# A decoder layer on one core: w_out staged four blocks at a time, gates in 32 rows, and loads read in the source's order

## The chip, the cores and the metric

The kernel runs on one core of a Trainium2 chip. It is one launch that computes one decoder layer for a prompt of 1024 tokens and for 8 single new tokens. The metric is the device time of one execution in microseconds, the median of the runs that were made. The core has a matmul engine (TensorE, PE in the profile, with its weight loads as PEld), three other compute engines (VectorE or DVE, ScalarE or ACT, GpSimd or POOL), and a queue of transfers that SyncE issues (SP). GpSimd issues transfers as well.

## The reference

The layer is `x = x + W_out(concat[RG-LRU branch, mLSTM branch])`, then a final norm. Both branches read the same normalised input through one projection `w_in` of 1024 to 7176 columns.

```
hn = rmsnorm(x, g_norm);  u = hn @ w_in
xa, za, uq, uk, uv, uo, zb, ui, uf = split(u)
yA, hA, bufA = rglru_branch(xa, ...)                  # conv of 4 taps, two gates, a scan over time
hB, C, n, m  = mlstm_seq(q, k, v, ig, lf, C0, n0, m0) # 4 heads, chunks of 128 tokens
yB = headnorm(sigmoid(uo) * hB) * g_mhead
merged = concat([yA * silu(za), yB * silu(zb)])
x = x + merged @ w_out;   y = rmsnorm(x, g_final)

# inside one chunk of the mLSTM, per head
b = cumsum(lf);  D = b_t - b_s + ig_s (causal);  g = b + m
m_t = max(g, max_s D);  w = exp(D - m_t);  P = w * (q k^T)
num = P v + exp(g - m_t) * (q C)
C_new = exp(b_L + m - m_L) * C + sum_s exp(b_L - b_s + ig_s - m_L) k_s v_s^T
```

The gate values `ig` and `lf` are one number for each token and head. From them come, for each token, the running maximum m and the factors that the chunks use. All in float32; the decode tokens do the same with one step from a given state of 8 x 4 matrices of 256 x 256.

## The kernel before

A float32 value is split into a high and a low part (`split`, lines 68 to 71: ScalarE copies the high part, VectorE subtracts it), and a product of two such values is three matmuls (`mm3`, lines 62 to 66). The order of the work in the source is written out by hand; a planner then places the instructions of each engine by the readiness it reckons for them, so an instruction can stand earlier in its engine's queue than in the source. A tile is released when its last reader is done, and a load into a reused tile waits for that.

**Projection.** `w_in` is worked through in 14 units (`UNITS`) of two 256-column blocks. Each unit is seven products (a Strassen-like scheme, `Q_P1` to `Q_P4`) of combinations of the input, kept in 14 slots of 128 x 2 x 1024 floats (`big(0)` to `big(13)`, two for each product), with combinations of the weights that `prep` makes in a ring of six tiles (`ws`). A product has two parts (`product` yields after each); after each part `pop_bg` runs a step of background work: the gates, the RG-LRU branch (`rgq`), the decode state updates (`dcq`). In the last unit the slots of a product come free as the product ends.

**Gates.** `gates` (lines 524 to 627) loads the parameters, takes log-sigmoids, and transposes the gate values of all tokens into 4 rows (heads) of 1024. Two scans along the row give the running maximum and, with a mask that restarts every 128 columns, the sums within a chunk. Four more row sets are stacked in a 128 x 1024 tile `stk` at rows 0, 32, 64 and 96 and transposed back eight times (L617). The factor between chunks goes to DRAM (`d_cs`) and is read back to all partitions. `d_alpha` holds a row for each head; each chunk and head later loads its piece to all partitions as W.

**Decode states.** `decode_steps` loads a state matrix C and a row v for each token and head, scales C on ScalarE (L881), adds the new outer product on VectorE (L883), and stores it.

**w_out and the output stage.** w_out is 16 blocks of 128 rows by 1024 columns, 0.5 MB each. `wo_load(n)` loads blocks n and n+1 into the `ws` ring. `wo_prep(n)` multiplies them with the decode rows (L1204, into `dec_o`) and splits them into the slot with the block's number (blocks 14 and 15 into the two raw tiles of the projection). Blocks 8 to 15 are scaled by `gm4` on the way (L1213, L1214). `wo_due` asks for blocks 0 to 7 after products 0 to 3 of the last unit; the rest is asked for in the code after the units and in the first steps of the output stage. There, 28 steps n (chunk and head) each run `m_k` (mask and exponent of W, splits), `m_a`, `m_b`; `fill` puts pieces of the output product (`out_part`, six or twelve matmuls a piece) between them. `o_load` loads the transposed RG-LRU rows rh and rl of a chunk.

Of the kernel before, what the change touches and what calls it, by code (L numbers as in the profile page):

```python
# [17 lines left out]
P = 128  # L18
# [31 lines left out]
def hymba_kernel(  # L50
# [17 lines left out]
    def split(hi, lo, src):  # L68

        A.copy(hi, src)  # L70
        V.tensor_tensor(lo, src, hi.bitcast(F32), op=ALU.subtract)  # L71

# [77 lines left out]
    d_alpha = dram.tile([NH, T], F32, name="d_alpha")  # L150
    d_cs = dram.tile([NH, NCH], F32, name="d_cs")
# [372 lines left out]
    def gates():  # L524
# [9 lines left out]
        stk = fp.tile([P, T], F32, tag="stk", name="stk")  # L534
        msk = fp.tile([NH, T], F32, tag="msk", name="msk")
        G.memset(msk, 1.0)
        G.memset(msk.rearrange("p (c l) -> p c l", l=L)[:, :, 0:1], 0.0)
        G.memset(stk, 0.0)
        dgb = fp.tile([P, NB, 8], F32, tag="dgb", name="dgb")
        ld(dgb, d_gd.partition_broadcast(P))  # L540
        yield
# [13 lines left out]
        V.scalar_tensor_tensor(lg, fx, 0.0, lg, op0=ALU.min, op1=ALU.subtract)  # L555
        lf = lg[:, 0:32].rearrange("p (c h) -> p c h", h=NH)
# [6 lines left out]
        V.tensor_scalar(gm4, PT[:, :, R_GM], 0.25, None, op0=ALU.mult)  # L563

        dgm = fp.tile([P, 2, NB, NH], F32, tag="dgm", name="dgm")
# [11 lines left out]
        rows = fp.tile([NH, 2, T], F32, tag="rows0", name="rows0")  # L577
        lfr, igr = rows[:, 0, :], rows[:, 1, :]
        for half in range(2):
            for src, dst in ((lf, lfr), (gs, igr)):  # L580
                pr = ps("s" if dst is lfr else "qp", [NH, 512])
                for q in range(4):
                    TE.transpose(pr[:, q * P:(q + 1) * P], src[:, half * 4 + q, 0:NH], idF)
                V.tensor_copy(dst[:, half * 512:(half + 1) * 512], pr)
            yield
        rows1 = fp.tile([NH, 2, T], F32, tag="rows1", name="rows1")
        mr, br = rows1[:, 0, :], rows1[:, 1, :]
        V.tensor_tensor_scan(mr, lfr, igr, 0.0, op0=ALU.add, op1=ALU.max)
        V.tensor_tensor_scan(br, msk, lfr, 0.0, op0=ALU.mult, op1=ALU.add)
        yield  # L590
        al = lfr
        V.tensor_tensor(al, br, mr, op=ALU.subtract)
        ld(d_alpha, al)
        stq(p_m[0, 0].rearrange("(h o) -> h o", o=1), mr[:, T - 1:T])
        V.tensor_tensor(br, igr, br, op=ALU.subtract)
        c3 = lambda t: t.rearrange("p (c l) -> p c l", l=L)
        sm = fp.tile([NH, 3, NCH], F32, tag="gsm", name="gsm")
        mpv, aL, csr = sm[:, 0], sm[:, 1], sm[:, 2]
        G.memset(mpv, 0.0)
        V.tensor_copy(mpv[:, 1:NCH], c3(mr)[:, 0:NCH - 1, L - 1])  # L600
        V.tensor_copy(aL, c3(al)[:, :, L - 1])
        V.tensor_tensor(csr, aL, mpv, op=ALU.add)
        A.activation(csr, csr, AF.Exp)
        ld(d_cs, csr)
        ld(cs_b, d_cs.partition_broadcast(P))
        yield
        V.tensor_tensor(c3(stk[0:4]), c3(al), mpv.unsqueeze(2).to_broadcast([NH, NCH, L]), op=ALU.add)
        V.tensor_copy(stk[32:36], br)
        V.tensor_tensor(c3(stk[64:68]), c3(br), aL.unsqueeze(2).to_broadcast([NH, NCH, L]), op=ALU.add)
        V.tensor_scalar(stk[96:100], mr, -1.0, None, op0=ALU.mult)  # L610
        for _ in range(14):
            yield
        for half in range(2):
            pk = ps(("s", "qp")[half], [P, 4, P])
            for q in range(4):
                c = half * 4 + q
                TE.transpose(pk[:, q, :], stk[:, c * P:(c + 1) * P], idF)  # L617
            s = slice(half * 4, half * 4 + 4)
            V.tensor_copy(be_t[:, s, :], pk[:, :, 32:36])
            A.activation(gi_t[:, s, :], pk[:, :, 0:4], AF.Exp)  # L620
            A.activation(de_t[:, s, :], pk[:, :, 64:68], AF.Exp)
            A.activation(em_t[:, s, :], pk[:, :, 96:100], AF.Exp)
            yield
# [51 lines left out]
    def rg_unit(jj):  # L675
# [10 lines left out]
        if jj == 3:  # L686
            rgq.extend([rg_final, lambda: None, rg_rows])
# [175 lines left out]
    def decode_steps(h):  # L863
# [12 lines left out]
        def token(b):  # L876
            i = h * NB + b

            def f():
                vb_, C = ds_.pop(("v", i)), ds_["C", i]  # L880
                A.mul(C, C, dGI[:, b, h:h + 1])  # L881
                for kb in range(2):
                    V.scalar_tensor_tensor(C[:, kb, :], vb_, st["kw"][:, kb, b:b + 1], C[:, kb, :],  # L883
                                           op0=ALU.mult, op1=ALU.add)
# [130 lines left out]
    def m_load(n):  # L1015
# [5 lines left out]
        ld(W, d_alpha[h:h + 1, ts_].rearrange("o t -> (o t)").partition_broadcast(P))  # L1021
# [20 lines left out]
    def m_k(n):  # L1042
# [5 lines left out]
        V.scalar_tensor_tensor(W, W, be_t[:, c, h:h + 1], maskT, op0=ALU.add, op1=ALU.min)  # L1048
# [132 lines left out]
    wo = []  # L1181
    dec_o = []

    oraw = {}

    def wo_load(n):

        for m in (n, n + 1):
            oraw[m] = ws([P, T], f"oraw{m}", F32)
            ld(oraw[m], w_out[0, m * P:(m + 1) * P, :])  # L1190

    def wo_prep(n):


        if n == 0:
            dec_o.append(ps("tr", [P, 512]))
        if n not in oraw:
            wo_load(n)
# [146 lines left out]
    def wo_due(q):  # L1345

        if q < 4:
            bg.append(lambda: wo_prep(2 * q))
# [26 lines left out]
    for n, (u, q) in enumerate(seq):  # L1375
# [4 lines left out]
        if u == last_u:  # L1380
            wo_due(q)
# [136 lines left out]
```

## Time and profile before

| | |
|---|---|
| median of the runs | 960.22 us (960.17 to 962.28) |
| the profiled execution | 960.01 us, of which the span of its instructions 958.2 us |
| granted TensorE clock, mean | 0.999 |
| TensorE busy | 930.4 us (97% of the span) |
| VectorE, ScalarE, GpSimd busy | 714.4, 583.9, 146.3 us |
| moved by DMA | 153.71 MB, mean 160 GB/s |

Rows of a timeline give start, duration, engine, line, operation, tiles written and read, and in brackets the idle time of the engine before it with what ended it. A count such as x4 means that as many records stand in the row. A float32 matmul leaves two records. Matmuls overlap, so their pace is read from the distance of their starts. Rows of waits give the waiting instruction, what it waited for, the time in total, how often, and the longest. TensorE's busy time is modelled, so small losses between matmuls don't appear as idle.

### The profile page before, as it was taken

To read this page: it belongs to the slowest core of one execution; us is meant where nothing else is said; L and a number is where in the kernel's file an instruction comes from. 1 tells how busy PE (TensorE), PEld (TensorE's weight loads), DVE (VectorE), ACT (ScalarE), POOL (GpSimd) and SP (SyncE) were. 2 spreads that over 40 slices of the span, in tenths; PEclk is the share of its full clock that TensorE was granted. 3 is DMA by queue.
4 is the path that set the end of the run, shared out by engine and by line. 5 is a ranking of instruction groups with operands and counts; after the bars stand their busy time and mean duration, and the time that the engine had idled before them with its cause. 6 is when DMAs were issued, how large, how long until landed. Compare 5 with 4: busy or idle time off the path is not lost.

```text
span 958.2 us, 15403 instructions
## 1 busy us (share of the span) xinstructions
PE 930.4 (97%) x5370; PEld 760.4 (79%) x5370; DVE 714.4 (75%) x1482; ACT 583.9 (61%) x1044; POOL 146.3 (15%) x258
## 2 busy tenths in 40 slices
PE   7999989999999999999999999999989999999997
PEld 7897767777787988787789998866557888888886
DVE  6876898879787878989787757686556676676664
ACT  6553446768676857677678664465546466455633
POOL 1111112112212122112212221010200100000020
PEclk9999999999999999999999999999999999999999
DMA  6431347345745465466636362434873654564361
GB/s 193 143 122 43 132 140 253 115 171 195 250 145 198 159 204 173 163 200 210 206 115 225 116 206 85 157 110 148 288 222 93 200 165 121 158 183 135 113 114 47
DMA packets 131363, 153.71 MB, mean 160 GB/s; under 512 B 15798, under 2 KB 110038, under 8 KB 131278
## 3 DMA queue, kind: packets, MB, share of 16 engines
q1 hardware_dynamic: 113558, 96.86, 33.8%
q0 software_dynamic: 17728, 55.87, 16.5%
q8 instruction: 42, 0.69, 0.3%
q14 instruction: 35, 0.29, 0.1%
HBM read 101.11 MB, written 51.65 MB: 159 GB/s over the span
## 4 chain that ended last, share of the span: by engine, by line
PE 70%; DVE 11%; DMA 10%; ACT 4%; issue 4%; SPq 1%; POOL 0%; ACTq 0%; DVEq 0%; POOLq 0%
PE ps_o L66 12%; PE ps_o L64 12%; PE ps_o L65 12%; PE ps_kv L64 7%; PE ps_kv L66 7%; PE ps_kv L65 7%; DMA Cb<-in_state_mlstm_C_dram 2%; PE ps_tr L227 2%; DMA W<-d_alpha 2%; PE ps_s L738 1%; PE ps_s L1068 1%; DVE wl L71 1%; DMA raw<-in_w_in_dram 1%; PE ps_tr L1204 1%; DMA oraw<-in_w_out_dram 1%
## 5 line engine op out<-in xcount | busy, mean ns | idle before, releaser
L71 DVE TENSOR_TENSOR wl<-raw,wh 128x1024 fp32r<-128x1024 f32 x91 | 111.0, 1220 | 28.4 <-ACT wh L70 18.6
L70 ACT CAST wh<-raw 128x1024 fp32r<-128x1024 f32 x91 | 95.2, 1047 | 60.0 <-PE ps_o L65 16.6
L64 PE MATMUL ps_kv<-cb_hi,wh 128*128 128x512 f32 x320 | 128.3, 401 | 0.5 <-ACT s L308 0.3
L66 PE MATMUL ps_kv<-cb_hi,wl 128*128 128x512 f32 x320 | 125.7, 393 | 0.0
L65 PE MATMUL ps_kv<-cb_lo,wh 128*128 128x512 f32 x320 | 125.1, 391 | 0.0
L64 PE MATMUL ps_o<-cb_hi,wh 128*128 128x512 f32 x240 | 95.0, 396 | 0.0
L66 PE MATMUL ps_o<-cb_hi,wl 128*128 128x512 f32 x240 | 94.0, 392 | 0.0
L65 PE MATMUL ps_o<-cb_lo,wh 128*128 128x512 f32 x240 | 93.6, 390 | 0.0
L64 PEld LDWEIGHTS ps_kv<-cb_hi,wh 128*128 128x128 f32 x320 | 60.1, 188 | 24.5 <-issue 5.5
L66 PEld LDWEIGHTS ps_kv<-cb_hi,wl 128*128 128x128 f32 x320 | 60.1, 188 | 15.6 <-issue 2.5
L65 PEld LDWEIGHTS ps_kv<-cb_lo,wh 128*128 128x128 f32 x320 | 60.2, 188 | 11.7
L64 PE MATMUL ps_kv<-wh,cb_hi 128*128 128x256 f32 x192 | 55.3, 288 | 0.0
L64 PE MATMUL ps_o<-wo,rh 128*128 128x512 f32 (+1 forms) x136 | 53.5, 394 | 1.7 <-DMA rh<-d_rm 1.7
L65 PE MATMUL ps_kv<-wl,cb_hi 128*128 128x256 f32 x192 | 54.3, 283 | 0.0
L66 PE MATMUL ps_kv<-wh,cb_lo 128*128 128x256 f32 x192 | 54.3, 283 | 0.0
L64 PEld LDWEIGHTS ps_o<-cb_hi,wh 128*128 128x128 f32 x240 | 45.1, 188 | 10.9 <-issue 1.7
L66 PEld LDWEIGHTS ps_o<-cb_hi,wl 128*128 128x128 f32 x240 | 45.0, 188 | 10.6 <-issue 0.8
L64 PE MATMUL ps_o<-wo,mh 128*128 128x512 f32 (+1 forms) x136 | 52.8, 388 | 0.0
L66 PE MATMUL ps_o<-wo,ml 128*128 128x512 f32 (+1 forms) x136 | 52.0, 382 | 0.8 <-DVE ml L71 0.8
L65 PEld LDWEIGHTS ps_o<-cb_lo,wh 128*128 128x128 f32 x240 | 45.1, 188 | 9.2
L66 PE MATMUL ps_o<-wo,rl 128*128 128x512 f32 (+1 forms) x136 | 52.0, 382 | 0.1
L65 PE MATMUL ps_o<-wo,rh 128*128 128x512 f32 (+1 forms) x136 | 51.8, 381 | 0.0
(469 smaller groups left out, 2534.2 us busy)
## 6 DMA issues: line engine op xcount, KB each, us to landing
raw<-in_w_in_dram SPq DMA_DIRECT2D x56, 512.0 KB
Cb<-in_state_mlstm_C_dram SPq DMA_DIRECT2D x32, 256.0 KB
out_dram<-Cb POOLq DMA_DIRECT2D x32, 256.0 KB, 4.3
qk<-d_qk SPq DMA_DIRECT2D x32, 256.0 KB
oraw<-in_w_out_dram SPq DMA_DIRECT2D x16, 512.0 KB
d_qk<-s POOLq DMA_DIRECT2D x24, 256.0 KB, 3.7
x<-in_x_prompt_dram SPq DMA_DIRECT2D x8, 512.0 KB
d_x<-s POOLq DMA_DIRECT2D x16, 256.0 KB, 2.7
```

Of the source, the lines that this page charges most:

```text
L64: TE.matmul(out, ah, bh, start=first, stop=False, skip_group_check=True)
L65: TE.matmul(out, ah, bl, start=False, stop=False, skip_group_check=True)
L66: TE.matmul(out, al, bh, start=False, stop=last, skip_group_check=True)
L70: A.copy(hi, src)
L71: V.tensor_tensor(lo, src, hi.bitcast(F32), op=ALU.subtract)
L227: TE.matmul(pz[32 * g:32 * g + 32, :], hnd[:, k, :], raws[u, k // 4][:, k % 4, :], start=k < 4, stop=k >= 4, skip_group_check=True)
L738: TE.matmul(pg, w[:, n, :], st["xx"][n], start=k == 0, stop=k == 1)
L1068: TE.matmul(S, qk[:, 2 + kb, :], qk[:, kb, :], start=kb == 0, stop=kb == 1)
L1204: TE.matmul(dec_o[0][32 * g:32 * g + 32, :], md, oraw[m][:, half * 512:(half + 1) * 512], start=n == 0, stop=n == 14, skip_group_check=True)
```

## The change

Gates: the 8 chunks and 4 heads become 32 rows of 128 columns. Scans run within a row; the maximum is carried between chunks by four scans over 8 values on one row; two small matmuls with ones bring the carried maximum to the rows and the factor between chunks to all partitions, instead of the trip through `d_cs`. The stack is one 128 x 128 tile and one transpose. The steps are spread over 13 background steps, one after each part, where there were 26, two after each part.

w_out: blocks 0 to 11 are loaded four at a time into slots 0 and 1 (free after the first product of the last unit), blocks 12 to 15 into the `ws` ring. `wo_dec` multiplies several pairs with the decode rows in one go, `wo_split` splits a pair into the slots two above its number (12 and 13 into the raw tiles, 14 and 15 into slots 0 and 1). `wo_due` is called after every part of the last unit; the first `o_load` stands in it. Ahead of the output stage stand five `fill` pieces in place of four.

Order: `pin` ties an instruction to the one before it in the source on the same engine, so it can't be placed ahead of that one; no wait is added. It is put on the two decode state operations, on the mask of W, and on ScalarE's part of the w_out split. The final rows of the RG-LRU branch come two empty steps later.

```diff
+    pin = tc.keep_in_program_order
-    d_alpha = dram.tile([NH, T], F32, name="d_alpha")
-    d_cs = dram.tile([NH, NCH], F32, name="d_cs")
+    d_alpha = dram.tile([NCH * NH, L], F32, name="d_alpha")
...
+        lgi = fp.tile([P, 2, 32], F32, tag="lgi", name="lgi")
+        V.scalar_tensor_tensor(lgi[:, 0], fx[:, 0:32], 0.0, lg[:, 0:32], op0=ALU.min, op1=ALU.subtract)
+        V.tensor_copy(lgi[:, 1].rearrange("p (c h) -> p c h", h=NH), gs[:, :, 0:4])
...
+        R = NCH * NH
+        pr = ps("qp", [R, 2, P])
+        for n in range(2):
+            TE.transpose(pr[:, n, :], lgi[:, n, :], idF)
...
+        V.tensor_tensor_scan(ml, lfr, igr, NEG, op0=ALU.add, op1=ALU.max)
+        V.tensor_tensor_scan(br, ones[0:R, :], lfr, 0.0, op0=ALU.mult, op1=ALU.add)
...
-                for q in range(4):
-                    TE.transpose(pr[:, q * P:(q + 1) * P], src[:, half * 4 + q, 0:NH], idF)
-        V.tensor_tensor_scan(mr, lfr, igr, 0.0, op0=ALU.add, op1=ALU.max)
-        V.tensor_tensor_scan(br, msk, lfr, 0.0, op0=ALU.mult, op1=ALU.add)
+        for n, t in enumerate((ml, br)):
+            TE.transpose(pe[:, n, :], t[:, L - 1:L], idF[:R, :R])
...
+        for h in range(NH):
+            V.tensor_tensor_scan(mrow[:, 1:, h], ch_(er[:, 1])[:, :, h], ch_(er[:, 0])[:, :, h], 0.0, op0=ALU.add, op1=ALU.max)
...
+        TE.matmul(pc[0:R, 0:1], mrow[:, 0:NCH, :].rearrange("p c h -> p (c h)"), ones[0:1, 0:1], start=True, stop=True)
+        TE.matmul(pc[:, 32:64], ones[0:1, :], er[:, 2], start=True, stop=True)
+        V.tensor_copy(cs_b.rearrange("p h c -> p c h"), ch_(pc[:, 32:64]))
...
-                TE.transpose(pk[:, q, :], stk[:, c * P:(c + 1) * P], idF)
+        TE.transpose(pk.rearrange("p g c h -> p (g c h)"), stk, idF)
...
-            rgq.extend([rg_final, lambda: None, rg_rows])
+            rgq.extend([rg_final, lambda: None, lambda: None, lambda: None, rg_rows])
...
-                A.mul(C, C, dGI[:, b, h:h + 1])
+                pin(A.mul(C, C, dGI[:, b, h:h + 1]))
...
+                    pin(V.scalar_tensor_tensor(C[:, kb, :], vb_, st["kw"][:, kb, b:b + 1], C[:, kb, :],
+                                               op0=ALU.mult, op1=ALU.add))
...
-        V.scalar_tensor_tensor(W, W, be_t[:, c, h:h + 1], maskT, op0=ALU.add, op1=ALU.min)
+        pin(V.scalar_tensor_tensor(W, W, be_t[:, c, h:h + 1], maskT, op0=ALU.add, op1=ALU.min))
...
+    def wo_load(n, slot=None):
+        for i, m in enumerate((n, n + 1)):
+            if slot is None:
+                oraw[m] = ws([P, T], f"oraw{m}", F32)
+            else:
+                if i == 0:
+                    pair = big(slot, [P, 2, T], f"oraw{m}", F32)
+                oraw[m] = pair[:, i]
             ld(oraw[m], w_out[0, m * P:(m + 1) * P, :])
+    def wo_dec(ns, first=False, last=False):
+        ms = [n + i for n in ns for i in range(2)]
+        for m in ms:
             md = mAd[:, m, :] if m < 8 else mB[0][:, m - 8, :]
             for half in range(2):
+                g = 2 * (m % 2) + half
                 TE.matmul(dec_o[0][32 * g:32 * g + 32, :], md, oraw[m][:, half * 512:(half + 1) * 512], ...)
+    def wo_split(n):
...
+                t = big(m + 2 if m < 12 else m - 14, [P, 2, T], f"wo{m}")
...
+                pin(A.mul(t[:, 0], raw, gm))
...
+    def wo_due(i):
+        if i in (1, 6, 11):
+            for slot in range(2):
+                wo_load({1: 0, 6: 4, 11: 8}[i] + 2 * slot, slot)
+        if i == 4:
+            wo_dec((0, 2), True)
+            wo_split(0)
+        if i == 5:
+            wo_split(2)
+        if i == 9:
+            wo_dec((4, 6))
+            wo_split(4)
+        if i == 10:
+            o_load(0)
+            wo_split(6)
+        if i == 12:
+            wo_load(12)
...
-    o_load(0)
     m_k(4)
-    wo_load(10)
-    wo_prep(8)
+    wo_load(14)
     fill(2)
-    wo_load(12)
-    wo_prep(10)
-    fill(2)
+    wo_dec((8, 10, 12))
+    for n in (8, 12, 10):
+        wo_split(n)
+    o_load(1)
+    fill(3)
+    wo_dec((14,), last=True)
+    wo_split(14)
```

More of the change, by code (lines that the diff above doesn't have):

```diff
@@ L533, in gates @@
         ld(m0b, st_m[0].partition_broadcast(P))
[L534 to L538, printed above, removed]
         dgb = fp.tile([P, NB, 8], F32, tag="dgb", name="dgb")
         ld(dgb, d_gd.partition_broadcast(P))
+        yield
         yield
@@ L609, in gates @@
[L609 to L623, printed above, removed]
+        V.tensor_scalar(stk[0:R], al, mp[:, 0:1], None, op0=ALU.add)
@@ new lines, in gates @@
+        V.tensor_copy(stk[R:2 * R], br)
+        V.tensor_scalar(stk[2 * R:3 * R], br, al[:, L - 1:L], None, op0=ALU.add)
+        V.tensor_scalar(stk[3 * R:4 * R], ml, -1.0, None, op0=ALU.mult)
+        yield
+        yield
+        pk = ps("s", [P, 4, NCH, NH])
+        TE.transpose(pk.rearrange("p g c h -> p (g c h)"), stk, idF)
+        V.tensor_copy(be_t, pk[:, 1])
+        A.activation(gi_t, pk[:, 0], AF.Exp)
+        A.activation(de_t, pk[:, 2], AF.Exp)
+        A.activation(em_t, pk[:, 3], AF.Exp)
@@ L1206, in wo_prep @@
+    def wo_split(n):
         for m in (n, n + 1):
             raw = oraw.pop(m)
[L1208 removed]
+            if m in (12, 13):
+                t = rawp.tile([P, 2, T], F32R, tag=f"raw{m - 12}", name=f"wo{m}")
+            else:
+                t = big(m + 2 if m < 12 else m - 14, [P, 2, T], f"wo{m}")
+            wo[m] = t
             if m < 8:
[L1210 removed]
+                pin(A.copy(t[:, 0], raw))
+                V.tensor_tensor(t[:, 1], raw, t[:, 0].bitcast(F32), op=ALU.subtract)
```

96 lines of the change are left out of this document (36 added, 60 removed).

## The prediction

> **What bounds the kernel now.** I read the page first, then the waits of TensorE, then busy time by stretch, then the timelines of the places that came out of that.
>
> ```profile
> span 958.2 us, 15403 instructions
> PE 930.4 (97%) x5370; PEld 760.4 (79%) x5370; DVE 714.4 (75%) x1482; ACT 583.9 (61%) x1044; POOL 146.3 (15%) x258
> PE 70%; DVE 11%; DMA 10%; ACT 4%; issue 4%; SPq 1%; POOL 0%; ACTq 0%; DVEq 0%; POOLq 0%
> ```
>
> TensorE is the bound: 97% busy, 27.8 us idle. An edit can gain in two ways only: it ends one of TensorE's waits, or it takes work off TensorE. The stretches (columns: length, then PE, PEld, DVE, ACT, POOL busy, clock, DMA share, GB/s) show where the idle time lies.
>
> ```profile
> 112.00:130.00 18.00, 15.66 (x85) 10.71 (x84) 17.67 (x31) 5.24 (x13) 3.14 (x8) 1.00 0.18 61
> 170.00:560.00 390.00, 389.13 (x2295) 318.23 (x2295) 326.01 (x538) 285.13 (x408) 77.40 (x127) 1.00 0.53 177
> 640.00:682.00 42.00, 40.09 (x173) 24.06 (x171) 27.64 (x50) 24.03 (x31) 4.42 (x9) 1.00 0.62 203
> 682.00:710.00 28.00, 24.46 (x120) 15.91 (x121) 14.60 (x25) 11.62 (x20) 3.18 (x6) 1.00 0.77 247
> 732.00:931.00 199.00, 197.34 (x1121) 169.60 (x1120) 135.50 (x423) 111.96 (x298) 19.53 (x34) 1.00 0.54 147
> 642.00:645.00 3.00, 2.87 (x15) 1.29 (x13) 2.27 (x9) 1.95 (x3) 0.54 (x1) 1.00 0.98 378
> ```
>
> Three stretches that the change touches lose 2.3 us (gates, 112 to 130, where VectorE is busy 17.67 of 18), 1.9 us (last projection unit, 640 to 682) and 3.5 us (crossing into the output stage, 682 to 710). From 170 to 560, where the decode steps run, only 0.9 us is lost; in the output stage to 931, 1.7 us. The waits of TensorE name the causes:
>
> ```profile
> PE ps_qp L64 <- ACT hh L1124: 3.0, 1, 3.0
> PE ps_s L617 <- DVE stk L609: 2.1, 1, 2.1
> PE ps_o L64 <- DMA rh<-d_rm: 1.7, 2, 1.4
> PE ps_s L822 <- DVE ORow L823: 1.3, 1, 1.3
> PE ps_s L738 <- ACT ig L692: 1.1, 3, 0.8
> PE ps_s L738 <- DVE xh L730: 1.0, 1, 1.0
> PE ps_tr L1204 <- DMA oraw<-in_w_out_dram: 0.4, 2, 0.2
> ```
>
> **The gates.** The 4-row form costs 16 small transposes (L583) and 8 full ones (L617) on TensorE, and long rows on VectorE: its time goes by the columns, 4 partitions or 128.
>
> ```profile
> L588 DVE TENSOR_TENSOR_SCAN rows<-rows x1: 2280/2280/2280, 116.5 to 116.5; 4x1024 f32<-4x1024 f32 x1
> L592 DVE TENSOR_TENSOR rows<-rows x1: 1211/1211/1211, 121.7 to 121.7; 4x1024 f32<-4x1024 f32 x1
> L608 DVE COPY stk<-rows x1: 683/683/683, 126.0 to 126.0; 4x1024 f32<-4x1024 f32 x1
> ...
> L765 DVE TENSOR_TENSOR_SCAN na<-rg,OC,ig 128x512 f32<-128x512 f32 x8 | 10.2, 1278 | 0.1
> 112.72 0.60 PE L583 MATMUL ps_s<-idF,gx 128*4 128x128 f32 x4 [0.28 <-DVE gx L555]
> 128.04 0.63 PE L617 MATMUL ps_s<-idF,stk 128*128 128x128 f32 x4 [2.06 <-DVE stk L609]
> 128.51 0.60 PE L617 MATMUL ps_qp<-idF,stk 128*128 128x128 f32 x4
> ```
>
> The scan is 2.2 ns a column at 4 rows and 2.5 at 128 rows, so a scan of 128 columns is near 0.3 us. Two long scans, four passes near 1.21 and six copies near 0.68 come to some 13.5 us of VectorE; the new form has two scans at 0.3, a copy of 256 columns and some eight passes of 128 columns at 0.15 to 0.35, four scans of 8 columns and a handful of single-row operations, about 4.5 us. VectorE is off the path except at one place: the last passes (L609) hold L617 for 2.06 us. That wait should go, since the passes end some 9 us of VectorE earlier. On TensorE, four transposes take 0.47 us (128.04 to 128.51); 24 in five visits, at 0.2 us of switching a visit (worked out for L1204 below, rounded down), are 3.8 us. The new form has 7 small ones in four visits, 1.6 us: -2.2. The gamma, decode-gate and rows steps keep their work. The d_cs round trip through DRAM (a store and a broadcast load on SP) becomes a matmul with ones, inside the seven. The removed memsets on GpSimd cost nothing here, since nothing waited for them. Sum: **-4.3**. Bounds: -6.4, if the freed VectorE also ends the 2.1 us of L738 waits that follow it, and -1, if the new chain of small steps (transpose, copy, scan, exponent, matmul) makes TensorE wait as long as L617 did and a bit more at its own transposes.
>
> **w_out: fewer and fuller visits.** Each 128-row block of w_out is multiplied once for the decode rows (L1204, two fp32 halves on two groups of 32 columns), and TensorE goes there 13 times:
>
> ```profile
> 671.21 0.39 PE L65 MATMUL ps_o<-cb_lo,wh 128*128 128x512 f32 x1
> 671.44 0.39 PE L66 MATMUL ps_o<-cb_hi,wl 128*128 128x512 f32 x1
> 671.76 1.05 PE L1204 MATMUL ps_tr<-oraw,mAd 128*32 128x512 f32 x4
> 672.74 0.50 PE L64 MATMUL ps_kv<-cb_hi,wh 128*128 128x512 f32 x1
> 673.08 0.39 PE L65 MATMUL ps_kv<-cb_lo,wh 128*128 128x512 f32 x1
> ...
> 679.66 1.06 PE L1204 MATMUL ps_tr<-oraw,mBd 128*32 128x512 f32 x8
> ...
> 686.36 1.92 PE L1204 MATMUL ps_tr<-oraw,mBd 128*32 128x512 f32 x8
> ```
>
> The pace of the big matmuls is 0.23 us (671.21 to 671.44). From 671.44 to 673.08 pass 1.64 us where two of them would take 0.46: a visit of one block costs 1.19. At 679.66 two blocks side by side take the time of one; at 686.36 two blocks in turn take 0.87 more. So the work proper is 0.87, the switching 0.32, and blocks pair up only when both have landed. Now: eight single visits for blocks 0 to 7 (9.5 us) and five for 8 to 15, one of them double (6.8): 16.3 us. The change loads four blocks at once and multiplies them together: at best eight pairs in four visits, 8 x 0.87 + 4 x 0.32 = 8.2, a gain of 8.1. At worst the blocks still come one at a time: 0. The likely value turns on arrival. The load for blocks 0 to 3 is issued after part 1 of the last unit and used after part 4; a part is 12 matmuls, 2.7 us, so there are 8.2 us.
>
> ```profile
> 640.41 0.81 SPq L1190 DMA_DIRECT2D oraw<-in_w_out_dram  x2
> ...
> 644.09 1.04 ACT L70 CAST wo<-oraw 128x1024 fp32r<-128x1024 f32 x1 [0.47 <-DMA oraw<-in_w_out_dram]
> 646.58 1.03 ACT L70 CAST wo<-oraw 128x1024 fp32r<-128x1024 f32 x1
> ```
>
> The first of two blocks issued at 640.41 was in use 3.7 us later. A block is 0.52 MB; at the 378 GB/s of 642 to 645 each further one takes 1.4 us, so four are in after about 7.9 us. That is just inside the cover, for the first two batches. I take -4 for blocks 0 to 7 (5.4 at best, one visit more) and -1 for 8 to 15, whose loads meet the other transfers of the crossing: **-5**. [...]
>
> **The crossing, 675 to 710.** What is late there is ScalarE, held by a block of w_out, and the transposed rows rh:
>
> ```profile
> 698.98 1.15 ACT L1213 ACTIVATE wo<-oraw,gm 128x1024 fp32r<-128x1024 f32 x1 [5.06 <-DMA oraw<-in_w_out_dram]
> 700.03 0.39 ACT L70 CAST qh<-qk 128x256 fp32r<-128x256 f32 x1
> ...
> 700.85 0.47 ACT L1124 ACTIVATE hh<-ps_qp,gi_t 128x257 f32<-128x257 f32 x1
> ```
>
> The scaling of a block waits 5.06 us for its load with qh, Ch and hh behind it; hh is the one that TensorE waits for (3.0). Kept in the source's order, the scaling no longer stands ahead of earlier work, and the loads start sooner. In the source rh is loaded three product parts earlier, ahead of blocks 8 to 15, instead of behind ten of the loads: its 1.7 should go. What comes late next: six blocks must be in before the third visit. They are asked for at parts 11 and 12 and need 10.6 us by the same rate; 5.4 us of product and 2.7 us of output matmuls cover them, so 2.5 us is left open. -3.0 - 1.7 + 2.5: **-2.2**. Bounds: -5 (all of it, with the 0.4 of L1204) and +4 (nothing gained, and rh of the second tile late behind 3 MB).
>
> **The tail.** The source now does three fills of output matmuls ahead of the steps where it did two, so one fill of six matmuls (1.4 us) is missing at the end, where it covered the last normalisation. It costs 0 if the crossing would have idled for it, 1.4 if not: **+0.7**.
>
> **The other pins.** The order of W, of C and of v on ScalarE and VectorE:
>
> ```profile
> L1048 DVE SCALAR_TENSOR_TENSOR W<-W,be_t,maskT 128x128 f32<-128x128 f32 x32 | 11.2, 350 | 46.5 <-DMA W<-d_alpha 46.5
> L1049 ACT ACTIVATE W<-W 128x128 f32<-128x128 f32 x32 | 9.9, 309 | 35.0 <-DVE W L1048 34.9
> ACT Cb L881 <- DMA Cb<-in_state_mlstm_C_dram: 10.3, 11, 2.8
> DVE Cb L883 <- DMA vbc<-d_dv: 8.3, 4, 5.2
> ```
>
> VectorE stands 46.5 us for W, but TensorE idles 1.7 us in that whole stage and 0.9 us in the decode stage. So this time is covered by matmuls: **0**, with -2.5 as the most to be had and +3 as the price if a pinned instruction comes late behind slower ones. The later rg_rows (two empty steps) may end the 1.3 us of L822: **0**, bound -1.3.
>
> Sum: -4.3 - 5 - 2.2 + 0.7 = -10.8. The profiled execution took 960.01 us (span 958.2 and 1.8 around it), 0.2 below the median of 960.22, so the sum stands for either: **949.2 us**. Its own range is 944.5 to 954.5.
>
> **Rivals.**
> 1. *Only the gates pay.* The blocks still arrive singly and the crossing keeps its waits under other names, because it moves the same 8.4 MB at 203 to 247 GB/s. 960.0 - 4.3 + 0.7 = 956.4. For it: the DMA shares of 0.62 and 0.77. Against: one 3 us burst reached 378 GB/s, so the transfers are held by issue and not by rate.
> 2. *The bounds add up.* VectorE's 9 us also end the L738 waits (-2.1 more), the pairs reach 8.1 (-3.1 more), the crossing is clean (-2.8 more): 960.0 - 18.8, about 941.
> 3. *Slower: the two staging buffers serialise the loads.* A batch can be asked for only when the batch before has been multiplied and split. At 177 GB/s, the mean of the decode stretch, a block takes 3.0 us and a batch 3.7 + 8.9 = 12.6; the cover is 8.2, so TensorE stands 4.4 us before each of three visits: 13.2. With no gain left at the crossing: 960.0 - 4.3 - 5 + 13.2 = 963.9. It decides once a batch takes over 11.3 us (three stalls of 3.1 eat the 9.3). Against: the burst above.
> 4. *Slower: the pinned W comes too late.* Mask (0.35) and exponent (0.31) of W then follow one another inside each of 27 steps instead of ahead of it: 17.8 less 10.8, 967. Against: W is asked for one step before its use.
> 5. *The pins do nothing*, as they tie an instruction to its predecessor only and leave later ones free to pass: this is within the forecast, which counts on one of them (hh).
>
> **Chances.** Forecast 0.45, rival 1 0.23, rival 2 0.17, rival 3 0.10, rival 4 0.05. A measurement of this kernel can tell about 0.3% (2.9 us) from no change. Rival 1 lies at that border, so a quarter of it counts as no change or worse: faster 0.79, same 0.08, slower 0.13. The range 940 to 959.5 leaves out the two slower rivals and the edge of the second.
>
> **What would show it.** L617 and L609 gone and TensorE's idle time in the gates' stretch under 0.5 us; four to six visits of L1204 with eight or more records each, taking 9 to 12 us together; no wait of TensorE on hh or rh over 1 us at the crossing; the wait of W on VectorE shorter with TensorE's idle time of the output stage unchanged. Wrong would be: long waits of L1204 on the loads (rival 3), TensorE waiting for ph or for the exponent of W (rival 4), or the same 13 visits (rival 1).

## The result, and the profile after

The changed kernel took **949.12 us** (median of four, 948.28 to 951.9), the kernel before beside it 961.25 us (960.17 to 963.24): a ratio of 0.9877, 95% interval 0.9848 to 0.9905. The prediction was 949.2 us. The total came out almost exactly, but its terms did not: what w_out and the crossing were to give together (7.2 us) came out about 5 us larger, and the decode stage, priced at nothing, lost 5.7 us.

The page of the changed kernel: span, busy time by engine, and the chain of work that ended last.

```profile
span 946.5 us, 15380 instructions
PE 927.4 (98%) x5355; PEld 763.1 (81%) x5355; DVE 711.1 (75%) x1488; ACT 583.2 (62%) x1041; POOL 144.6 (15%) x254
PE 89%; DVE 5%; DMA 2%; ACT 2%; issue 1%; SPq 0%; DVEq 0%; ACTq 0%
```

TensorE's share of the chain rose from 70% to 89%, and the DMA's fell from 10% to 2%: most of what is left is matmul. The same stretches as before the change (length, then PE, PEld, DVE, ACT, POOL busy, clock, DMA share, GB/s):

```profile
112.00:130.00 18.00, 17.74 (x85) 11.24 (x85) 14.70 (x53) 6.68 (x16) 4.04 (x9) 1.00 0.38 123
170.00:560.00 390.00, 388.14 (x2241) 313.91 (x2240) 326.29 (x533) 281.90 (x401) 78.84 (x128) 1.00 0.55 179
640.00:682.00 42.00, 41.92 (x211) 29.49 (x213) 34.03 (x73) 30.33 (x43) 5.23 (x10) 1.00 0.73 255
682.00:710.00 28.00, 28.00 (x156) 22.10 (x149) 17.92 (x36) 13.88 (x28) 2.94 (x6) 1.00 0.78 235
710.00:930.00 220.00, 218.11 (x1259) 188.47 (x1258) 154.50 (x468) 124.19 (x329) 22.04 (x38) 1.00 0.50 142
```

TensorE's idle time fell from 2.3 to 0.3 us in the gates, from 1.9 to 0.1 in the last unit, and from 3.5 to 0 at the crossing. In the decode stretch it rose, from 0.9 to 1.9 us, and busy time hides more than that. Both traces have 1448 matmuls of line 64, up to k = 871 in the same sequence but for one pair, so the start of the k-th one in each tells where time is lost or won (worked out from the two traces, us). Behind that some pieces stand in another order. The row for 960 therefore takes the same matmul in both traces (k = 961 before), and the row for 1080 is good to 1 or 2 us only:

```
k       where                         before   after    after-before   since the row above
0       first combination               9.83    9.80      -0.03
120     start of the projection        72.27   74.23      +1.95           +1.98
240     behind the gates              171.86  169.09      -2.77           -4.72
840     behind most of the decode     548.89  551.84      +2.95           +5.72
960     before the last unit          614.56  616.50      +1.94           -1.01
1080    in the output stage           721.05  710.83     -10.22          -12.16
1447    last one                      951.10  939.30     -11.79           -1.57
```

So the gates gave 4.7 us, the last unit and the crossing about 12, the decode stage lost 5.7, and 2.0 us went at the very start, where the change edits nothing. The 1.0 us between k = 840 and 960 goes with TensorE's wait of 1.3 us at L822, which is gone. The visits for the decode products of w_out in the changed kernel:

```profile
647.07 1.04 PE L1213 MATMUL ps_tr<-oraw,mAd 128*32 128x512 f32 x2
648.58 1.92 PE L1213 MATMUL ps_tr<-oraw,mAd 128*32 128x512 f32 x14
664.26 1.93 PE L1213 MATMUL ps_tr<-oraw,mAd 128*32 128x512 f32 x16
679.98 2.78 PE L1213 MATMUL ps_tr<-oraw,mBd 128*32 128x512 f32 x24
687.02 1.06 PE L1213 MATMUL ps_tr<-oraw,mBd 128*32 128x512 f32 x8
```

There are 5 visits in place of 13. From the first start of a visit to the start of the next other matmul they take 8.4 us together, where they took 15.3. In the 15.3 are 1.4 us in which TensorE waits for rh behind the visit at 679.66, and the switching into and out of a visit is in neither number. Counted as the prediction counts a visit, with the switching and without waits (the distance from the matmul before to the one behind the next, less the usual pace), they take 9.4 us where they took 16.6.

Next, one batch of the decode states' products. Before the change:

```profile
314.99 0.61 PE L902 MATMUL ps_qp<-Cb,qsel 128*4 128x256 f32 x8
```

and after it:

```profile
313.02 0.60 PE L910 MATMUL ps_qp<-Cb,qsel 128*4 128x256 f32 x4
...
315.62 0.59 PE L910 MATMUL ps_qp<-Cb,qsel 128*4 128x256 f32 x2 [0.85 <-DVE Cb L891]
...
316.69 0.59 PE L910 MATMUL ps_qp<-Cb,qsel 128*4 128x256 f32 x2
```

A batch of eight records on four column groups has become three pieces, each as long as the whole was. This happens to three of the 16 batches (at 313, 526 and 555 us), and two more stretch to 1.45 and 1.50 us. By the distance of starts, the 16 batches take 13.8 us where they took 8.8.

The 2.0 us at the start belong to the granted clock (PEclk is the number after the engines' columns):

```profile
16.30:19.70 3.40, 3.40 (x18) 3.40 (x18) 2.39 (x3) 0.00 (x0) 0.00 (x0) 0.50 0.06 14
```

For 3.4 us TensorE ran at half its clock, which costs 1.7 of the 2.0 us. The profiled execution of the kernel before had no such stretch at its start (clock 1.00 in its first 40 us), but five of those profiled below did (0.91 or 0.96 there); two in whose profile it is missing (without the kept W, and with w_out and W alone, 1.00 there) start the projection within 0.1 us of the kernel before.

### The profile page after: what moved, and what is told of

Its sections match the earlier page's. It is cut to its first block, busy times and chain, and to the rows that moved or that the text cites. A ratio compares the mean times of both kernels' runs of the same rounds, so it can differ in the third digit from the quotient of the medians.

```text
span 946.5 us, 15380 instructions
## 1 busy us (share of the span) xinstructions
PE 927.4 (98%) x5355; PEld 763.1 (81%) x5355; DVE 711.1 (75%) x1488; ACT 583.2 (62%) x1041; POOL 144.6 (15%) x254
## 4 chain that ended last, share of the span: by engine, by line
PE 89%; DVE 5%; DMA 2%; ACT 2%; issue 1%; SPq 0%; DVEq 0%; ACTq 0%
PE ps_o L64 14%; PE ps_o L66 14%; PE ps_o L65 14%; PE ps_kv L64 11%; PE ps_kv L65 10%; PE ps_kv L66 10%; PE ps_tr L228 3%; PE ps_s L746 2%; PE ps_s L1076 1%; PE ps_qp L910 1%; DMA raw<-in_w_in_dram 1%; PE ps_qp L64 1%; PE ps_tr L1213 1%; PE ps_qp L65 1%; PE ps_qp L66 1%
## 5 line engine op out<-in xcount | busy, mean ns | idle before, releaser
L64 PE MATMUL ps_o<-wo,mh 128*128 128x512 f32 (+1 forms) x136 | 53.2, 392 | 1.0 <-ACT mh L70 1.0
L65 PE MATMUL ps_o<-wo,mh 128*128 128x512 f32 (+1 forms) x136 | 51.6, 380 | 0.0
```

Of the source, the lines that this page charges most:

```text
L64: TE.matmul(out, ah, bh, start=first, stop=False, skip_group_check=True)
L65: TE.matmul(out, ah, bl, start=False, stop=False, skip_group_check=True)
```

## The experiments

Ratios are to the kernel before, run beside each kernel. "Kept" means kept in the source's order by `pin`.

### Which part gave what

**The gates alone.** The kernel before with the gates' steps of the change, the layout of `d_alpha` and one background step a part in unit 1:

```diff
-    bg.extend([lambda: next(gg, None)] * 26 + [rd_open])
+    bg.extend([lambda: next(gg, None)] * 13 + [rd_open])
-            pop_bg(2 if u == 1 or u == last_u else 1, 1, part % DEC[1 if u >= DEC[0] else 2] == 1)
+            pop_bg(2 if u == last_u else 1, 1, part % DEC[1 if u >= DEC[0] else 2] == 1)
```

> The kernel before with the 32-row gates alone (their steps, the changed layout of the gates' row in DRAM, half as many steps per part in unit 1); w_out and the order as before. Theory A, the gates gain what the changed kernel showed between its 117th and 169th us, and keep it to the end: 3.6 to 4.7 us, 957.4 to 958.5 us beside a kernel before of 962.1. Rival B, the wait at the crossing swallows it, since it waits for VectorE behind its loads and not for TensorE: 960 to 962 us.

Measured: 958.05 us, ratio 0.9962 (0.9943 to 0.9980). The gain of 3.7 us is there by itself; theory A holds. In its trace TensorE idles 4.2 us less between k = 120 and 240 than before, and works 0.4 us less.

**The kept W alone.**

```diff
-        V.scalar_tensor_tensor(W, W, be_t[:, c, h:h + 1], maskT, op0=ALU.add, op1=ALU.min)
+        pin(V.scalar_tensor_tensor(W, W, be_t[:, c, h:h + 1], maskT, op0=ALU.add, op1=ALU.min))
```

> The kernel before with the mask instruction on W kept in order, and nothing else. Theory A, before the change this instruction stands early in VectorE's order, VectorE waits for the transfer of W 46.5 us in 24 times, and TensorE's waits for hh, z and ORow at the crossing are waits behind it; kept in order it waits for under 8 us and the crossing gains alone: 6 to 10 us, 952 to 956 us beside 962.1. Rival B, the order pays only beside the staged w_out, because ScalarE still waits for the raw rows there: 959 to 962 us.

Measured: 959.45 us, ratio 0.9974 (0.9959 to 0.9989), 2.3 us. That lies in B's range. The wait of VectorE for W is gone altogether, yet TensorE still waits for hh; what was gained lies in the output stage, where TensorE's idle time from 710 us up to the last 25 us falls from 1.8 us to nothing. ScalarE's timeline at the crossing:

```profile
698.85 1.15 ACT L1215 ACTIVATE wo<-oraw,gm 128x1024 fp32r<-128x1024 f32 x1 [4.85 <-DMA oraw<-in_w_out_dram]
...
700.72 0.47 ACT L1126 ACTIVATE hh<-ps_qp,gi_t 128x257 f32<-128x257 f32 x1
```

and the wait of TensorE there:

```profile
PE ps_qp L64 <- ACT hh L1126: 2.2, 1, 2.2
```

ScalarE stands 4.85 us for a block of w_out with hh behind it, just as before the change. Before the change no instruction on W stands in the way there: VectorE has none between 621 and 706 us, and where it stands still longest at the crossing it waits for ScalarE's scaling of that block. Two rows of VectorE in the kernel before:

```profile
700.16 1.28 DVE L1214 SCALAR_TENSOR_TENSOR wo<-oraw,gm,wo 128x1024 fp32r<-128x1024 f32 x1 [4.92 <-ACT wo L1213]
...
706.14 0.34 DVE L1048 SCALAR_TENSOR_TENSOR W<-W,be_t,maskT 128x128 f32<-128x128 f32 x1
```

**The staged w_out alone,** without any kept instruction and with the gates as before:

```diff
-                pin(A.copy(t[:, 0], raw))
+                A.copy(t[:, 0], raw)
-                pin(A.mul(t[:, 0], raw, gm))
+                A.mul(t[:, 0], raw, gm)
```

(this against the changed `wo_split`; `wo_load`, `wo_dec`, `wo_due` and the fills are the changed ones, and the later rows of the RG-LRU branch are in).

> The kernel before with the staged w_out alone (the changed loads, products and splits, the later rg_rows; no instruction kept in order, gates as before). Theory A, the visits of the decode products of w_out shrink from 16.3 to some 9 us, and TensorE's waits behind W on VectorE (some 8 us in the kernel without the kept W) stay: 953 to 957 us beside 962.1. Rival B, the loads are the cause of the waits at the crossing too: 948 to 951 us. Rival C, the visits shrink but the waits grow by as much: 960 to 963 us.

Measured: 951.54 us, ratio 0.9899 (0.9877 to 0.9921). The gain of 10.2 us is a little more than A said and less than B. The visits shrink to 8.4 us, the same as in the changed kernel, but TensorE still waits at the crossing, now behind VectorE. The mask on W, which ran at 706 us before, now stands at 691 us, ahead of its data. VectorE's timeline there:

```profile
691.36 0.35 DVE L1050 SCALAR_TENSOR_TENSOR W<-W,be_t,maskT 128x128 f32<-128x128 f32 x1 [4.73 <-DMA W<-d_alpha]
```

and TensorE's waits between 600 and 720 us:

```profile
PE ps_o L66 <- DVE ml L71: 2.5, 1, 2.5
PE ps_qp L64 <- ACT hh L1126: 1.9, 1, 1.9
```

**Both, with the gates as before.** The staged w_out (as above) and the kept W.

> The kernel before with the staged w_out and the mask instruction on W kept in order, the gates as before. Alone the two gave 951.5 and 959.5 us beside 961.8. Theory A, the wait at the crossing stands behind both the raw rows of w_out on ScalarE and W on VectorE, so taking only one away leaves it: together they give more than their sum, 944.5 to 947 us, with no wait of TensorE for hh between 600 and 720 us. Rival B, they only add up, and what the three parts give beyond it needs the gates: 948.5 to 950 us.

Measured: 942.83 us, ratio 0.9796 (0.9772 to 0.9821). Alone the two parts gave 2.3 and 10.2 us, 12.5 in sum; together they give 2.04%, 19.6 us. So they do more than add up, and even more than theory A reckoned. TensorE at the crossing:

```profile
600.00:720.00 120.00, 120.00 (x620) 90.98 (x619) 86.58 (x183) 66.98 (x124) 11.79 (x23) 1.00 0.56 186
```

It never idles there. So two things can hold the crossing: ScalarE behind a block of w_out, as before the change, and VectorE (with ScalarE behind it) behind a row of W, once w_out is staged and the planner has put the mask earlier. TensorE waits 5.1 us there before the change, 3.9 with W alone kept, 4.4 with w_out alone staged, and not at all with both.

### What each kept instruction is worth in the changed kernel

**Without the decode's two.**

```diff
-                pin(A.mul(C, C, dGI[:, b, h:h + 1]))
+                A.mul(C, C, dGI[:, b, h:h + 1])
-                    pin(V.scalar_tensor_tensor(C[:, kb, :], vb_, ..., op1=ALU.add))
+                    V.scalar_tensor_tensor(C[:, kb, :], vb_, ..., op1=ALU.add)
```

> The changed kernel with the keeping in order taken off the two instructions of a decode token (the scaling of C on ScalarE, the adding of v on VectorE), all else as changed. Its 16 batches of decode products take 13.8 us on TensorE where they took 8.8 us before the change: three are split in pieces of 4, 2 and 2 records, two are stretched to 1.45 and 1.50 us. Theory A, the two kept instructions do this: all 16 batches are whole again, 8.8 us, the six extra visits save their switching too (some 0.3 us each, as the w_out visits showed), so 949.1 - 5.0 - 1.5 = 942.5 us, within 941 to 945. Rival B, the loss in the decode stage comes from the planner's other choices (the shorter gates, the startup): the batches may be whole but the waits on C and v come back on ScalarE and VectorE and reach TensorE elsewhere: 947.5 to 951 us.

Measured: 945.94 us, ratio 0.9826 (0.9800 to 0.9853). All 16 batches are whole and take 8.8 us again, and the stretch from k = 240 to 840 that lost 5.7 us loses 2.0. A is right on the cause, but the time stays 1 us above its range: part of what the kept order had been good for comes back. ScalarE's timeline:

```profile
464.37 0.72 ACT L889 ACTIVATE Cb<-Cb,dGI 128x512 f32<-128x512 f32 x1 [4.98 <-DMA Cb<-in_state_mlstm_C_dram]
465.12 0.58 ACT L309 COPY s<-ps_kv 128x512 f32<-128x512 f32 x1
```

and TensorE's two longest waits:

```profile
PE ps_kv L64 <- ACT s L309: 2.7, 2, 1.5
PE ps_s L1182 <- ACT W L1057: 2.1, 1, 2.1
```

ScalarE stands 4.98 us for a state matrix with a copy out of PSUM (where TensorE writes its results) behind it, and TensorE waits 2.7 us for such copies, where the changed kernel waits 0.7. The 2.1 us for W come from one late transfer at 728 us, which other kernels here show too.

**Without the kept W.**

```diff
-        pin(V.scalar_tensor_tensor(W, W, be_t[:, c, h:h + 1], maskT, op0=ALU.add, op1=ALU.min))
+        V.scalar_tensor_tensor(W, W, be_t[:, c, h:h + 1], maskT, op0=ALU.add, op1=ALU.min)
```

> The changed kernel with the keeping in order taken off the mask instruction on W alone; TensorE's own order stays the same, VectorE's changes in the last third. Theory A, the wait for W stood on VectorE but TensorE never waited behind it: 949.1 us within 0.8, with a wait for W back on VectorE (over 5 us in all) and TensorE's idle time the same within 0.5 us. Rival B, the output stage gained its 1.6 us from this: 950.2 to 951.5 us, with waits of TensorE for W or for what VectorE does after it.

Measured: 958.55 us, ratio 0.9973 (0.9947 to 0.9998). Against 0.9877 of the changed kernel this one line is worth 9 us, far outside what either theory said. In the traces the two spans differ by 8.7 us, of which 7.3 are idle time of TensorE: 3.7 in the crossing (640 to 710), the rest before and behind it. The waits of VectorE and TensorE:

```profile
DVE W L1056 <- DMA W<-d_alpha: 41.2, 21, 5.8
PE ps_qp L64 <- ACT hh L1132: 3.0, 1, 3.0
PE ps_s L1182 <- DVE kl L1086: 2.4, 1, 2.4
```

and the timeline of VectorE and ScalarE at the crossing:

```profile
697.52 0.35 DVE L1056 SCALAR_TENSOR_TENSOR W<-W,be_t,maskT 128x128 f32<-128x128 f32 x1 [5.79 <-DMA W<-d_alpha]
697.91 0.31 ACT L1057 ACTIVATE W<-W 128x128 f32<-128x128 f32 x1 [6.50 <-DVE W L1056]
698.12 0.39 ACT L70 CAST qh<-qk 128x256 fp32r<-128x256 f32 x1
...
698.94 0.47 ACT L1132 ACTIVATE hh<-ps_qp,gi_t 128x257 f32<-128x257 f32 x1
```

The mask on W stands on VectorE ahead of its data and waits 5.79 us. The exponent of W waits on ScalarE behind it for 6.50 us, then come qh, Ch and hh: the same queue that before the change stood behind a block of w_out. The wait of 3.0 us for hh is as long as it was then.

**Without the kept split of w_out.** The edit is the one shown for the staged w_out alone, here in the changed kernel.

> The changed kernel with the keeping in order taken off the high half of the w_out split on ScalarE alone. Theory A, the crossing gained because the raw rows are loaded earlier, not because of the order: 949.1 us within 0.8, the rows of w_out wait for at most 2.5 us on ScalarE, TensorE nowhere. Rival B, the order does it: without it splits come ahead of their rows again, ScalarE waits for w_out some 4 us or more and TensorE for hh or z behind it, 951.5 to 954 us.

Measured: 947.77 us, ratio 0.9856 (0.9827 to 0.9885), not to be told from the changed kernel. ScalarE waits 2.9 us for the rows in all (1.9 with the order kept, and A allowed 2.5), and TensorE nowhere at the crossing. The early loads matter, not the order: A.

**Without any kept instruction.**

> The changed kernel with none of the four instructions kept in order: only the 32-row gates, the staged w_out and the later rg_rows are left of the change. Theory A, the kept order is worth nothing but its cost in the decode stage: as the kernel without the decode's two, 942.5 us, within 941 to 945. Rival B, the kept order of W and w_out is worth something in the last third: 945 to 949 us, slower than the kernel without the decode's two alone by over 1.5 us.

Measured: 950.47 us, ratio 0.9878 (0.9846 to 0.9911), 4.5 us above the kernel without the decode's two. A falls; B is right that the order is worth something in the last third, and too low. The kept instructions together thus change nothing that can be seen (0.9877 with all of them). Taken away singly, W's costs 9 us and the decode's two give 3 to 5, so the single prices don't simply add.

**Only W's kept.**

> The changed kernel with only the mask instruction on W kept in order: gates and w_out staged as changed, the decode's two and the split's high half left to the planner. Theory A, of the kept instructions W's is the only one that pays: as the kernel without the decode's two, 945.9 us within 1.5, and at least 4 us under the kernel with none kept (950.5). Rival B, the kept split pays beside it: 947.5 to 950 us, with waits for the raw rows of w_out on ScalarE.

Measured: **942.03 us**, ratio 0.9804 (0.9779 to 0.9828). This beats both kernels, and the one without any kept instruction by more than 7 us; it lies under A's range too. It is lower than the kernel without the decode's two by 3.9 us, but this is not shown to be the split's doing: TensorE waits for the late W in that kernel's profile and not in this one's, and two more stretches at half clock stand in it, which cost 3.4 us together (clock 0.91 against 0.96 in the first 40 us, 0.99 against 1.00 from 710 to 930 us). Beside the kernel with the gates as before (0.9796) the ratio is the same, so once w_out and W are in, the gates' 3.7 us can't be seen in the medians. In the profiles the 3.7 us are partly there: between k = 120 and 240 this kernel gains 3.1 us on the kernel before, and the one with the old gates loses 0.8; at the end the difference is 0.7 us, with 1.7 us of half clock at the start of this one alone (clock 0.96 in its first 40 us, 1.00 in the other's).

### Prices taken by themselves

**A batch of decode products in two halves,** in the kernel with only W kept; the second half is issued one step later.

```diff
-            def products():
+            def products(g0=0):
-                for g in range(4):
+                for g in (g0, g0 + 1):
+                if g0 == 0:
+                    late.append(lambda: products(2))
+                    return
```

> The kernel with only W's instruction kept in order (942.0 us), where each of its 16 batches of decode products is issued in two halves, the two blocks of one token in one step and those of the other in the next; nothing is kept in order for it and no product comes ahead of what it reads. Theory A, what costs in the decode stage is the breaking of a batch: a whole one took 0.55 us, a piece of 4 records 0.53 us, so 32 pieces take 17.0 us in place of 8.8, and 16 switches more at some 0.3 us: +8.2 to +13 us, 950 to 955 us. Rival B, it was the wait of TensorE for the adds and not the breaking: 942 to 944 us.

Measured: 954.06 us, ratio 0.9909 (0.9880 to 0.9937). For 16 breaks that is 12.0 us by the medians, 10 by the ratios, and 11.4 in the traces between k = 240 and 840. The first batch of this kind in the place shown above:

```profile
314.83 0.60 PE L910 MATMUL ps_qp<-Cb,qsel 128*4 128x256 f32 x4
...
318.43 0.60 PE L910 MATMUL ps_qp<-Cb,qsel 128*4 128x256 f32 x4
```

Each half costs what the whole did. The pieces take 16.9 us, 8.1 more; the rest is put down to switching. No product waits here for its data, so the breaking itself is the cost: A, at 0.6 to 0.75 us a break. The changed kernel's six extra pieces come to 3.8 to 4.5 us by that price, and the two stretched batches add 1.8, against the 5.7 us lost.

**Blocks of w_out apart,** in the kernel with only W kept: within a visit the even blocks come first, then the odd ones.

```diff
-        ms = [n + i for n in ns for i in range(2)]
+        ms = [n + i for i in range(2) for n in ns]
```

> The kernel with only W's instruction kept in order (942.0 us), with the decode products of w_out in another sequence within a visit: first the even blocks, then the odd ones, so that blocks that follow each other write the same two column groups. Theory A, two neighbours in four column groups run side by side, and only two groups do here except where the even ones meet the odd ones: 0.87 us of work is not shared once in each batch of two pairs (two batches) and twice in the batch of three: 4 x 0.87 = +3.5 us, 945.5 us, within 944.5 to 947. Rival B, the gain of the visits came from fewer switches alone: 942.0 us within 1.2, visits as long as before.

Measured: 945.41 us, ratio 0.9816 (0.9788 to 0.9843), 1.2 us above the other by the ratios and 3.4 by the medians, with intervals that overlap. The visits give the clear answer. Two of them in this kernel:

```profile
660.88 1.94 PE L1213 MATMUL ps_tr<-oraw,mAd 128*32 128x512 f32 x16
676.62 3.66 PE L1213 MATMUL ps_tr<-oraw,mBd 128*32 128x512 f32 x24
```

and in the kernel with the blocks in turn:

```profile
658.94 1.92 PE L1213 MATMUL ps_tr<-oraw,mAd 128*32 128x512 f32 x16
674.66 2.78 PE L1213 MATMUL ps_tr<-oraw,mBd 128*32 128x512 f32 x24
```

A's time is met and its reason is not: four blocks take the same time in either sequence; only the visit of six grows, by 0.88 us, one unit of work. What the medians differ by beyond that lies outside the visits: this execution has a wait of 3.0 us for a copy out of PSUM at 464 us and a stretch at half clock after it.

**Two steps of output product at the start in place of three,** in the kernel with only W kept.

```diff
     o_load(1)
-    fill(3)
+    fill(2)
```

> The kernel with only W's instruction kept in order (942.0 us), with two steps of the output product in place of three behind the splits ahead of the loop, so that one more is left for its end. Theory A, the wait of 1.0 us for mh near the end is that missing step: it goes, 941 us. Rival B, the stage at the crossing needs the third step to cover its splits: a wait of the same size or more there, 942 to 945 us.

Measured: **941.38 us**, ratio 0.9776 (0.9750 to 0.9801). The wait that the changed kernel has at its end,

```profile
PE ps_o L64 <- ACT mh L70: 1.0, 1, 1.0
```

is gone, and no wait of TensorE replaces it from 700 us to the end. The place is as A said; the 0.65 us between the medians is too little to be told from nothing. This is the fastest of the kernels that were run, 1.0% under the changed one by ratios whose intervals don't meet.

## Why the prediction was right in sum, and wrong in its terms

**Gates, -4.3.** Right in size (4.7 in the traces, 3.7 for the gates alone), and the wait of 2.06 us of L617 is gone as foreseen, but the two halves of the term are not. Between k = 120 and 240 TensorE idles 4.1 us less (4.4 to 0.3): beside L617's wait the 2.1 us for xh and ig are gone, which the term left to rival 2. Its own work shrinks by 0.6 us, where fewer transposes and visits were to save 2.2. The sum is near because these two errors cancel.

**w_out visits, -5.** Too small: 16.6 to 9.4 us, -7.2. The step that failed is the allowance for blocks that arrive late. Only one visit broke, and into two records and 14. The full -8.1 that is named there as the best case, eight pairs in four visits, was nearer than the cautious figure.

**Crossing, -2.2.** The step "the scaling no longer stands ahead of earlier work, and the loads start sooner" found the blocker that was there, and missed the one that came in its place: the mask on W. All 5.1 us of waits there are gone in the changed kernel, but 3.7 to 4.4 us of waits stand there as soon as either the early loads or the kept W is taken away. Of the two halves of that step only the loads count: without the kept split TensorE doesn't wait there either. The +2.5 for the third batch of loads did not come: TensorE waits for no block.

**Other pins, 0.** This term failed twice. The step "VectorE stands 46.5 us for W, but TensorE idles 1.7 us in that whole stage, so this time is covered by matmuls" is right for the order of the kernel before: kept alone, W gives 2.3 us, within the 2.5 named as most. It doesn't hold for the order that the planner makes once w_out is staged. There the mask stands ahead of its data at the crossing unless it is kept, and keeping it is worth 9 us. The sign named for it, "TensorE's idle time of the output stage unchanged", came true in number (1.7 us from 732 to 931 before, 1.9 from 710 to 930 after), but 1.0 of the 1.9 is the tail's wait.

On the other side, the decode's two kept instructions cost 3.7 us between k = 240 and 840, against the kernel without them, and the whole stretch lost 5.7 against the kernel before, where +3 was the bound: the price was sought in waits, and lies mostly in broken batches. How they break the traces show. Before the change the additions to C run far ahead of the products; kept in order, they come late:

```profile
L883 DVE SCALAR_TENSOR_TENSOR Cb<-vbc,kw,Cb x64: 451/480/486, 146.7 to 535.3; 128x256 f32<-128x256 f32 x64
L891 DVE SCALAR_TENSOR_TENSOR Cb<-vbc,kw,Cb x64: 475/480/486, 183.3 to 555.6; 128x256 f32<-128x256 f32 x64
```

(The first row is of the kernel before, the second of the changed one; both give the start of the first and the last.) A batch started 11 to 55 us after its last addition had ended; in the changed kernel it starts 5.7 us behind it at most. In five of the 16 batches the last addition ends 0.9 to 2.9 us after the batch has begun, and these are the three broken and the two stretched ones. In the kernel without the decode's two the lead is back, 11 to 60 us, and so are the whole batches.

**The later rg_rows, 0.** The wait of 1.3 us of L822, named as the bound, is gone in the changed kernel; the same wait is 1.2 us in the kernel without the kept W, which has the later rows too, so the later rows alone are not shown to end it.

**Tail, +0.7.** Right: 1.0 us of wait for mh, gone with one step moved back.

**The rivals.** Rival 1 and the slower ones, 3 and 4, did not occur: W kept in order came in time but for 0.9 us, and no batch of loads stalled. Rival 2 came true for the visits and the crossing, and for the gates in the waits alone. Its 941 is what the kernel with only W kept (942.0) and the one with the tail mended (941.4) show, both without the decode's two kept instructions. The changed kernel's profile misses it by the 5.7 us of the decode stage and the 2.0 us of its start. So the forecast was met because a gain of 12 us in the last third, where 7.2 were forecast, was eaten by a loss that was priced at nothing. That the two came out alike is luck.

**Left open.** Keeping ScalarE's scaling of C but not VectorE's addition, or issuing the products a step later with both kept, might join whole batches with the shorter waits for copies out of PSUM; neither was tried. What the kept split of w_out costs or gives is under what these runs can tell.

## What to carry to other kernels

A wait that is read from the old trace is a price in the old order only. When an edit takes one wait away and the planner orders the work anew, another late load can be put into the same place: read the crossing again in the new order, and test the parts of a change together as well as one by one, since here one alone gave 2.3 us, the other 10.2 and both 19.6. An instruction kept in the source's order protects what is behind it and delays what depends on it: keep it where its data come late (W), and check how far ahead of the matmuls that read its result it runs before keeping it elsewhere (C). When a sum comes out right, compare the parts by the start times of the same instruction in both traces before believing the terms.

## What the runs showed of the hardware

**Half clock after a wait.** In three kernels a stretch with a clock of 0.50 begins 2.0 to 3.1 us after the beginning of a TensorE wait: 6.7 us of it behind the wait of 3.5 us in the kernel with the gates alone (from 697.0 us on), 3.4 us behind the wait of 2.2 us in the kernel before with the kept W alone (from 701.0 us on), and 3.3 us behind the wait of 3.0 us in the one with the blocks apart:

```profile
463.90:467.00 3.10, 0.08 (x2) 0.01 (x1) 0.44 (x2) 1.35 (x3) 0.00 (x0) 0.99 0.31 110
467.00:470.30 3.30, 3.30 (x8) 2.62 (x9) 2.33 (x6) 3.25 (x5) 0.72 (x1) 0.50 0.32 109
```

Such a stretch of 3.4 us, with TensorE at work all through it, costs half of that, 1.7 us, so by these numbers a wait of 2 us can cost nearly 4 (an estimate). The changed kernel, whose TensorE waits at most 1.1 us at a time, has a clock of 1.00 from 19.8 to 944.7 us. Not every longer wait is followed by half clock: the kernel before waits 3.0 and 2.1 us and has 1.00 from 7 to 955.8 us, and the kernel without the kept W waits 3.0 us between 600 and 720 us and 2.4 us between 720 and 760, and has 1.00 in the stretches from 682 to 710 and from 710 to 930 us. What decides it is not shown by these runs.

**Blocks on the same column groups, one behind the other.** Four blocks took 1.92 us in turn and 1.94 apart, where two blocks that follow each other write the same column groups. Six blocks, three in a row on the same groups, took 3.66 us apart and 2.78 in turn, 0.88 us more. This is read from these two sizes only; why the second grows and the first doesn't is not shown.
